# Splitting 20 weight pieces of k, r and v in the first FFN of a Griffin and RWKV-7 trunk, by way of DRAM

## The chip, the cores and the metric

The kernel runs on one core of a Trainium2 chip. The metric is the time of one execution on the device in microseconds (us); the median over runs counts. The engines are named as the profile names them: PE (TensorE, matrix products), PEld (its weight loads), DVE (VectorE), ACT (ScalarE), POOL (GpSimd) and SP (SyncE, which here only issues DMAs).

## The reference, cut to what matters

Two layers over 512 tokens of 1024 channels: a Griffin RG-LRU block, a gated conv-MLP (the first FFN, `D_FF` = 3072), an RWKV-7 time mixing, and a second FFN. The change touches the first FFN and the projections of the time mixing.

```python
def _conv_ffn(x, norm, w_up, conv_w, conv_b, w_down):
    h = _rmsnorm(x, norm)
    u = jnp.einsum('btd,df->btf', h, w_up)
    gate = _causal_dwconv(u[..., :D_FF], conv_w, conv_b)
    hid = jax.nn.gelu(gate, approximate=True) * u[..., D_FF:]
    return jnp.einsum('btf,fd->btd', hid, w_down)

def _rwkv7_block(x, norm, mix, w_rkv, ...):
    h = _rmsnorm(x, norm)
    xx = jnp.pad(h, ((0, 0), (1, 0), (0, 0)))[:, :-1] - h
    xs_rkv = jnp.stack([h + xx * mix[0], h + xx * mix[1], h + xx * mix[2]])
    rkv = jnp.einsum('sbtd,sde->sbte', xs_rkv, w_rkv)
    r, k, v = rkv[0], rkv[1], rkv[2]
...
```

## The kernel before

All products are made in float32 precision out of three products in the PE's faster float32r: every operand is split into a rounded part `hi` and a rest `lo`, and `mm3` (L54) adds `hi*hi`, `hi*lo` and `lo*hi` in PSUM. Activations are split once; the weights come from DRAM as float32 in pieces of 128 x 1024 (512 KB). `plan_weights` lists all pieces in the order of their use. `weights_load` (L161) fetches the next ones into a `raw` tile with a DMA on SP's queue (L166; for some pieces a second, summing DMA on POOL's queue, L168), `weights_split` (L172) makes `wh` on ACT (L94) and `wl` on DVE (L97), and `next_weights` hands a split piece to the product and keeps two pieces loading and one split ahead. All these tiles come from one pool `b4` of 21 buffers of 4 KB per partition, in which mixes, selections and other tiles of that size live too.

`project_gen` runs a product over four blocks of output: 8 passes of 3 matmuls for a piece in each block's turn, 24 matmuls of 512 columns a piece. After each step it calls `background`, which advances generators in the list `tasks` (three lanes) at a given rate, so that work of other stages is spread between the products.

The first FFN (`ffn(0)`, 157 to some 526 us) works on 12 pairs of 256 hidden channels. Pairs 0 to 2, 4, 6, 8 and 10 are `Whole`: four products G0, U0, G1, U1 (gate and up, halves of the 1024 inputs). Pairs 3, 5, 7, 9 and 11 are `Halves`, a form with seven products of half size (1, 5, 6, 2, 7, then 4, 3). The gate's product lands in `gpad`, of which two tiles take turns (n % 2), goes through the convolution `cv` (L688, L690) into `ge` (two buffers), and is multiplied into the hidden tile `hid`. After the products up to 7 of each divided pair a product down (`down`, L869 by way of `project`) adds four pieces of `w_down` into x, with products 4 and 3 run in between after its first piece.

The time mixing begins with the small products of `rwkv_lora` (`lwa`, `lg`), then `rwkv_lora_k` makes the first half of k (with `l2w`, `l2a` for decay and a among it) and `rwkv_krv` the second half of k, both halves of r, and part of v. Beside them `prepare` makes norms and decays in ACT and DVE (`AR`, `BK`, with small products `ssq`, `sst`, `rec`, `knb`), and `solve` inverts 32 x 32 triangles (`aab` on PE, `A`, `D`, `X` on DVE, then `XN`, `LT` and the product `m1p`). `back` is a selection matrix, transposed on PE from `sel`, which POOL fills (L1133, L1139) at the beginning of `rwkv_krv`; it is used only in `knb`. The order on each engine is set by a scheduler that places instructions by its own estimates; the order of the code gives the dependencies, and the reuse of buffers.

## Time and profile before

| what | value |
| --- | --- |
| median of 3 runs | 1293.43 us (1292.26 to 1294.64) |
| profiled execution | 1295.77 us, span 1294.1 us |
| granted PE clock, mean | 0.996 |
| stretch 157 to 526 us (first FFN): PE, DVE, ACT busy | 369.0, 256.3, 158.6 us of 369 |
| stretch 526 to 707 us (lora, k, r, first of v) | 172.6, 158.4, 113.4 us of 181 |
| stretch 707 to 870 us (chunks, product out) | 154.3, 121.4, 101.7 us of 163 |
| stretch 870 to 1294 us (second FFN) | 417.8, 271.4, 180.3 us of 424 |
| DMA: share and rate in the four stretches | 0.49, 129 GB/s; 0.27, 82; 0.21, 64; 0.44, 120 |

A stretch is read in us from the first instruction. Busy times are sums of the instructions' spans on an engine. Consecutive matmuls overlap, so that a PE that is busy all the time may still differ in how many products it makes. A wait is the idle time of an engine in front of an instruction and is put down to what ended last.

### The profile page before, as it was taken

What the parts mean: (1) busy time and instruction counts of PE and PEld (TensorE: products, weight loads), DVE (VectorE), ACT (ScalarE), POOL (GpSimd) and SP (SyncE); (2) the same over time, 40 slices, a digit from 0 to 9 for tenths busy, and PEclk for the clock granted to TensorE, in tenths of its full rate; (3) what the DMA queues carried; (4) which work ended last, traced back from release to release, by engine and by line L of the source; (5) the groups of instructions that cost most, each with busy time, mean ns of one, the idle gap of its engine ahead of it and who ended that gap; (6) DMA issues with size and microseconds to landing.
All of it is one profiled execution on the core that took longest, in us unless ns stands there. A gap on an engine that the chain in (4) does not pass through costs nothing.

```text
span 1294.1 us, 22380 instructions
## 1 busy us (share of the span) xinstructions
PE 1267.5 (98%) x9259; PEld 1069.2 (83%) x9259; DVE 931.4 (72%) x1412; ACT 664.6 (51%) x1070; POOL 104.6 (8%) x142
## 2 busy tenths in 40 slices
PE   9999999999999999999899999899999999999998
PEld 8777888989888888877678887778889898988886
DVE  5998678757666666788999867778866565666653
ACT  6797455434334343468845468655644343343432
POOL 3000001010101000010002031210010101010100
PEclk9999999999999999999999999999999999999999
DMA  7312344545454553422212122132354544545431
GB/s 222 110 58 90 98 129 100 161 100 166 95 176 85 179 99 101 157 71 76 82 38 87 51 61 83 44 99 77 107 110 148 113 162 99 171 91 178 97 133 65
DMA packets 117829, 141.37 MB, mean 109 GB/s; under 512 B 10138, under 2 KB 91748, under 8 KB 117600
## 3 DMA queue, kind: packets, MB, share of 16 engines
q1 hardware_dynamic: 100528, 122.44, 30.0%
q0 software_dynamic: 16624, 16.47, 8.4%
q8 instruction: 72, 1.18, 0.4%
q10 hardware_dynamic: 576, 1.05, 0.2%
q14 instruction: 29, 0.24, 0.1%
HBM read 135.41 MB, written 4.52 MB: 108 GB/s over the span
## 4 chain that ended last, share of the span: by engine, by line
PE 85%; DVE 8%; ACT 4%; issue 2%; POOL 0%; DMA 0%; POOLq 0%; ACTq 0%; DVEq 0%
PE acc L54 26%; PE accU L54 12%; PE accG L54 12%; PE accA L54 9%; PE accF L54 4%; PE acc L845 3%; PE acc L844 3%; PE acc L843 3%; PE accD L54 2%; DVE wl L97 1%; PE acc L1244 1%; PE s L1412 1%; DVE AR L1102 1%; DVE mt L965 1%; PE pd L1494 1%
## 5 line engine op out<-in xcount | busy, mean ns | idle before, releaser
L97 DVE TENSOR_TENSOR wl<-raw,wh 128x1024 fp32r<-128x1024 f32 (+1 forms) x161 | 195.5, 1220 | 128.1 <-ACT wh L94 107.8
L94 ACT CAST wh<-raw 128x1024 fp32r<-128x1024 f32 (+1 forms) x161 | 165.9, 1042 | 195.5 <-PE acc L54 54.5
L54 PE MATMUL accG<-xs,wh 128*128 128x512 f32 x448 | 138.8, 391 | 0.0
L54 PE MATMUL accU<-xs,wh 128*128 128x512 f32 x448 | 138.7, 391 | 0.0
L54 PE MATMUL acc<-hid,wh 128*128 128x512 f32 x384 | 119.8, 395 | 0.0
L744 DVE TENSOR_TENSOR lo<-raw,hi 128x1024 fp32r<-128x1024 f32 x70 | 85.5, 1222 | 39.4 <-PE accU L54 32.0
L743 ACT CAST hi<-raw 128x1024 fp32r<-128x1024 f32 x70 | 73.6, 1053 | 60.7 <-PE accU L54 25.3
L54 PEld LDWEIGHTS accG<-xs,wh 128*128 128x128 f32 x448 | 83.6, 188 | 17.4
L54 PEld LDWEIGHTS accU<-xs,wh 128*128 128x128 f32 x448 | 83.7, 188 | 17.1
L54 PE MATMUL accG<-xs,wl 128*128 128x512 f32 x224 | 87.3, 390 | 0.0
L54 PE MATMUL accU<-xs,wl 128*128 128x512 f32 x224 | 87.3, 390 | 0.0
L54 PEld LDWEIGHTS acc<-hid,wh 128*128 128x128 f32 x384 | 71.3, 187 | 16.7
L54 PE MATMUL accA<-xt,hi 128*128 128x256 f32 x480 | 83.4, 277 | 0.0
L54 PE MATMUL acc<-xs,wh 128*128 128x512 f32 x256 | 81.1, 399 | 0.0
L690 DVE SCALAR_TENSOR_TENSOR cv<-gpad,pv,cv 128x512 f32<-128x512 f32 x96 | 69.1, 747 | 12.3 <-ACT cv L688 11.8
L845 PE MATMUL acc<-wl,hid 128*128 128x512 f32 (+1 forms) x200 | 77.2, 386 | 0.0
L844 PE MATMUL acc<-wh,hid 128*128 128x512 f32 (+1 forms) x200 | 77.0, 385 | 0.0
L843 PE MATMUL acc<-wh,hid 128*128 128x512 f32 (+1 forms) x200 | 76.7, 383 | 0.0
L54 PE MATMUL acc<-hid,wl 128*128 128x512 f32 x192 | 75.0, 395 | 0.0
L54 PEld LDWEIGHTS accA<-xt,hi 128*128 128x128 f32 x480 | 73.2, 188 | 0.9
L54 PE MATMUL accA<-xt,lo 128*128 128x256 f32 x240 | 66.3, 276 | 0.0
L168 POOL DMA_DIRECT2D raw<-in_ffn_w_up_dram x20 | 25.7, 1287 | 478.5 <-DMA raw<-in_ffn_w_up_dram 283.6
(411 smaller groups left out, 2943.4 us busy)
## 6 DMA issues: line engine op xcount, KB each, us to landing
raw<-in_ffn_w_up_dram SPq DMA_DIRECT2D x106, 512.0 KB, 3.9
raw<-in_ffn_w_down_dram SPq DMA_DIRECT2D x48, 512.0 KB, 3.9
raw<-in_ffn_w_up_dram POOLq DMA_DIRECT2D x30, 512.0 KB, 5.9
raw<-in_rwkv_w_rkv_dram SPq DMA_DIRECT2D x24, 512.0 KB, 3.7
raw<-in_lru_w_in_dram SPq DMA_DIRECT2D x16, 512.0 KB, 4.2
raw<-in_lru_w_out_dram SPq DMA_DIRECT2D x8, 512.0 KB, 3.8
raw<-in_rwkv_w_out_dram SPq DMA_DIRECT2D x8, 512.0 KB, 3.4
xd<-x SPq DMA_DIRECT2D x8, 256.0 KB, 2.0
```

Source lines behind the costliest of these rows:

```text
L54: mm = lambda *a, **kw: self.nc.tensor.matmul(ps, *a, skip_group_check=more, **kw)
L94: put = (self.nc.vector.tensor_copy if dve else self.nc.scalar.copy)(hi, src)
L97: self.nc.vector.tensor_tensor(lo, src, hi.bitcast(F32), ALU.subtract)
L168: self.nc.gpsimd.dma_start(raw, more, accum_op=ALU.add)
L690: nc.vector.scalar_tensor_tensor(cv, pair.gp[:, e, j : j + T], cw(j), cv, ALU.mult, ALU.add)
L743: nc.scalar.copy(hi, f[p])
L744: tt(lo, f[p], hi.bitcast(F32), ALU.subtract)
L843: nc.tensor.matmul(ps, hh[:, s], wh[:, k, m], start=kk == 0, stop=False)
L844: nc.tensor.matmul(ps, hl[:, s], wh[:, k, m], start=False, stop=False)
L845: nc.tensor.matmul(ps, hh[:, s], wl[:, k, m], start=False, stop=kk == blocks - 1)
L965: nc.vector.scalar_tensor_tensor(mt[:, 1:], h[:, cb, : T - 1], self.vec("rwkv_mix", i * 8 + cb), mt[:, 1:], ALU.mult, ALU.add)
L1102: nc.vector.tensor_tensor_scan(AR[b // 4][:, b % 4, c, C : 3 * C], kp, sg[:, c * P : (c + 1) * P], 0.0, ALU.mult, ALU.add)
```

## The change

The plan marks 20 pieces as made ahead: the 8 of k, the 8 of r and the first 4 of v (`AHEAD`). A generator `split_ahead` fetches one of them per step on SP's queue into a tile `early`, splits the one fetched in the step before into `eh` (ACT) and `el` (DVE), and stores the parts split a step earlier to DRAM with two DMAs on POOL's queue. It is pushed to lane 1 in the first FFN, behind products up to 7 of pair 3, and advances by 0.19 at each of the 16 steps of a product down (3 steps in each), and by 0.25 at each of the 8 calls of a whole pair (2 in each); before the last product down the rest is done at once. Later `weights_load` takes `wh` and `wl` of such a piece from DRAM with two DMAs on POOL's queue (float32 in DRAM, float32r in the tile), and `weights_split` has nothing to do for it.

The room for `early` (2 x 4 KB) is made in the first FFN by one `gpad` and one buffer of `ge` in place of two. Around the products down, pieces are split earlier (`between`, `then`), and `back` is made in the third step of `prepare`.

```diff
--- before.py
+++ after.py
@@ -29,6 +29,8 @@
 WARM2 = 20
 WARM = 14
 
+AHEAD = 20
+
 HALVES = (3, 5, 7, 9, 11)
 
 PARAMS = [
@@ -145,6 +147,7 @@
         full(I["lru_w_in"][0], [2, 3, 0, 1])
         full(I["lru_w_out"][0], [0, 1])
         ffn(0)
+        self.ahead = range(len(plan), len(plan) + AHEAD)
         for i in (1, 0):
             full(I["rwkv_w_rkv"][0, i], [0, 1])
         for g in range(4):
@@ -155,19 +158,46 @@
                 add(I["rwkv_w_out"][0], h * 512, g * 256, 4)
         ffn(1)
         self.plan = plan
-        self.loaded, self.splitted = {}, {}
+        self.loaded, self.splitted, self.stored = {}, {}, {}
         self.n_load = self.n_split = self.n_used = 0
 
     def weights_load(self, upto):
         while self.n_load < min(upto, len(self.plan)):
             i = self.n_load
             src, k, _, more = self.plan[i]
+            if i in self.stored:
+                self.loaded[i] = tuple(self.b4(F32R, (k, D // k), f"{part}{i}") for part in ("wh", "wl"))
+                for t, d in zip(self.loaded[i], self.stored[i]):
+                    self.nc.gpsimd.dma_start(t, d)
+                self.n_load += 1
+                continue
             raw = self.b4(F32, (k, D // k), f"raw{i}")
             self.nc.sync.dma_start(raw, src)
             if more is not None:
                 self.nc.gpsimd.dma_start(raw, more, accum_op=ALU.add)
             self.loaded[i] = raw
             self.n_load += 1
+
+    def split_ahead(self, pool):
+
+        raws, parts = {}, {}
+        n = self.ahead.stop
+
+        for i in range(self.ahead.start, n + 2):
+            if i < n:
+                src, k = self.plan[i][:2]
+                raws[i] = pool.tile([P, k, D // k], F32, tag="early", name="early", bufs=2)
+                self.nc.sync.dma_start(raws[i], src)
+            if i - 2 in parts:
+                k = self.plan[i - 2][1]
+                self.stored[i - 2] = [self.dram.tile([P, k, D // k], F32, name=f"{part}d{i - 2}") for part in ("wh", "wl")]
+                for t, d in zip(parts.pop(i - 2), self.stored[i - 2]):
+                    self.nc.gpsimd.dma_start(d, t.bitcast(F32))
+            if i - 1 in raws:
+                k = self.plan[i - 1][1]
+                parts[i - 1] = [self.b4(F32R, (k, D // k), f"{part}{i - 1}") for part in ("eh", "el")]
+                self.split(raws.pop(i - 1), *parts[i - 1])
+            yield 1
 
     def weights_split(self, upto, pin=False):
         while self.n_split < min(upto, len(self.plan)):
@@ -177,6 +207,10 @@
                 continue
             self.weights_load(i + 1)
             raw = self.loaded.pop(i)
+            if i in self.stored:
+                self.splitted[i] = raw
+                self.n_split += 1
+                continue
             k = self.plan[i][1]
             hi = self.b4(F32R, (k, D // k), f"wh{i}")
             lo = self.b4(F32R, (k, D // k), f"wl{i}")
@@ -236,7 +270,7 @@
         self.const = ctx.enter_context(tc.tile_pool(name="const", bufs=1))
         self.psum = ctx.enter_context(tc.tile_pool(name="psum", bufs=1, space=PSUM))
         self.xsp = ctx.enter_context(tc.tile_pool(name="xsp", bufs=1))
-        dram = ctx.enter_context(tc.tile_pool(name="dram", bufs=1, space=DRAM))
+        dram = self.dram = ctx.enter_context(tc.tile_pool(name="dram", bufs=1, space=DRAM))
         self.xd = dram.tile([P, KB, T], F32, name="xd")
         self.tgd = dram.tile([160, T], F32, name="tgd")
         c = self.const
@@ -591,7 +625,7 @@
                 return pool.tile([P, n], dt, tag=tag, name=tag, bufs=bufs)
 
             rbs, norm = [], []
-            gpads = [pool.tile([P, 2, T + 2], F32, name=f"gpad{i}") for i in range(2)]
+            gpads = [pool.tile([P, 2, T + 2], F32, name=f"gpad{i}") for i in range(1 + l)]
             for u in gpads:
                 nc.vector.memset(u[:, :, 0:2], 0.0)
             late = []
@@ -676,12 +710,12 @@
             class Pair:
 
                 def __init__(pair, n):
-                    pair.n, pair.gp = n, gpads[n % 2]
+                    pair.n, pair.gp = n, gpads[n % len(gpads)]
                     pair.w, pair.bank, pair.s = {}, {}, {}
 
                 def gate(pair, e):
                     if not e:
-                        pair.ge = pool.tile([P, 2, T], F32, tag="ge", name="ge", bufs=2)
+                        pair.ge = pool.tile([P, 2, T], F32, tag="ge", name="ge", bufs=1 + l)
                     fb = 2 * pair.n + e
                     cv = t("cv", 2)
                     cw = lambda j: self.vec(f"ffn_conv_w{l}", j * FB + fb)
@@ -722,6 +756,7 @@
                                 tt(un, un, pair.ge[:, e], ALU.mult)
                             self.split(un, pair.hid[:, e, 0], pair.hid[:, e, 1])
                         self.background(1)
+                        self.background(0.25, 1)
 
             class Halves(Pair):
 
@@ -866,7 +901,7 @@
                             elif not g and c == pieces - 1:
                                 then()
 
-                        self.project(hids, ev, kb=blocks, join=2 if g else 1, rate=0.5 if final else 2, after=hook, x0=b0)
+                        self.project(hids, ev, kb=blocks, join=2 if g else 1, rate=0.5 if final else 2, rate1=0 if final else 0.19, after=hook, x0=b0)
 
             rooms = []
 
@@ -875,12 +910,27 @@
                     rooms.append(pool.tile([P, 2, 2, T], F32R, tag="xt", name="hx", bufs=4))
                 return rooms[-1][:, b % 2, 0], rooms[-1][:, b % 2, 1]
 
+            def between():
+                products((n, 3))
+                if n < 11:
+                    self.weights_split(self.n_used + 2)
+
+            def then():
+
+                if len(seq) > at[0]:
+                    self.weights_split(self.n_used + 2)
+                ahead(at[0] + 2)
+
             for n in range(3, 12, 2):
                 products((n, 7))
+                if n == 3 and not last:
+                    self.push(self.split_ahead(pool), 1)
                 if n == 11 and not last:
+                    while self.tasks[1]:
+                        self.background(1, 1)
                     self.norm_begin()
                     self.push(self.lora_weights())
-                down(n, 2 * n - 6, 4 if n < 11 else 8, lambda: products((n, 3)), lambda: ahead(at[0] + 2))
+                down(n, 2 * n - 6, 4 if n < 11 else 8, between, then)
             if not last:
                 after()
 
@@ -1139,11 +1189,15 @@
                     nc.gpsimd.memset(sel[hb, b, c : c + 1], 1.0)
             for b in range(KB):
                 nc.gpsimd.tensor_copy(selk[hb, b, e : e + 1], self.vec("rwkv_r_k", b)[hb])
-        psb = self.bank("back")
-        for j in range(4):
-            nc.tensor.transpose(psb[0:40, j * P : (j + 1) * P], sel[:, j, :], self.ident)
-        back = self.b4(F32R, (4 * P,), "back")[0:40]
-        nc.scalar.copy(back, psb[0:40, :])
+        backs = []
+
+        def selection():
+            psb = self.bank("back")
+            for j in range(4):
+                nc.tensor.transpose(psb[0:40, j * P : (j + 1) * P], sel[:, j, :], self.ident)
+            backs.append(self.b4(F32R, (4 * P,), "back")[0:40])
+            nc.scalar.copy(backs[0], psb[0:40, :])
+
         ppads = [pool.tile([P, NC, C + 1], F32, name=f"ppad{i}") for i in range(2)]
         for pp in ppads:
             nc.vector.memset(pp[:, :, 0:1], 1.0)
@@ -1167,6 +1221,8 @@
                 nc.scalar.activation(bytok(fac), a, AF.Identity, bias=self.oka[:, b : b + 1], scale=self.vec("rwkv_k_a", b))
                 nc.scalar.activation(pp[:, :, :, 1:], Lc, AF.Exp, scale=-DECAY_C)
                 yield 1
+                if g == 0 and j == 2:
+                    selection()
 
                 sqs.append(sq)
                 for i in (3, 0, 1, 2) if j == 3 else ():
@@ -1202,7 +1258,7 @@
                 b = g * 4 + j
                 Lc = self.inner(AR, b)
                 pb = self.bank("knb")
-                nc.tensor.matmul(pb, back[:, j * P : (j + 1) * P], rec, start=True, stop=True)
+                nc.tensor.matmul(pb, backs[0][:, j * P : (j + 1) * P], rec, start=True, stop=True)
                 nc.vector.scalar_tensor_tensor(Lc, Lc, self.nkk[:, b : b + 1], bytok(pb), ALU.mult, ALU.mult)
                 if j == 3:
                     self.done.add(("prepare", g))
```

The line numbers grow by 2 to 56 with this: L54 becomes L56, L94 and L97 become L96 and L99, L168 becomes L177, L748 becomes L783. `raw` keeps its name, and the new lines are L171 (loads of stored parts), L190 (fetch of `early`) and L195 (stores).

The first place is POOL's queue in the first FFN, from pair 3 to pair 5. Before, it holds summing transfers of divided pairs alone:

```order
L168 DMA raw_1900<-in_ffn_w_up_dram 128x4x256
L748 DMA raw_1893<-in_ffn_w_up_dram 128x4x256
L168 DMA raw_2423<-in_ffn_w_up_dram 128x4x256
L168 DMA raw_2428<-in_ffn_w_up_dram 128x4x256
L748 DMA raw_2421<-in_ffn_w_up_dram 128x4x256
```

And in the changed kernel, with the stores (`whd`, `wld` are the tiles in DRAM):

```order
L783 DMA raw_1891<-in_ffn_w_up_dram 128x4x256
L195 DMA whd_2395<-eh_2356 128x1024
L195 DMA whd_2479<-eh_2399 128x1024
L195 DMA wld_2396<-el_2357 128x1024
L195 DMA wld_2480<-el_2400 128x1024
L177 DMA raw_2439<-in_ffn_w_up_dram 128x4x256
L195 DMA whd_2573<-eh_2483 128x1024
L177 DMA raw_2444<-in_ffn_w_up_dram 128x4x256
L195 DMA wld_2574<-el_2484 128x1024
L195 DMA whd_2871<-eh_2577 128x1024
L195 DMA wld_2872<-el_2578 128x1024
L783 DMA raw_2437<-in_ffn_w_up_dram 128x4x256
```

Eight stores now stand ahead of and between the summing transfers of pair 5, where there were none.

The second place is PE at the second half of k. Before, `back` stands ahead of the first piece of that half (`acc_5265` is its first block):

```order
L54 MATMUL acc_4929<-mix,wh_5074 128x512 x2
L54 MATMUL acc_4929<-mix,wl_5075 128x512
L1144 MATMUL back<-ident,sel 40x128 x4
L54 MATMUL acc_5265<-mix,wh_5080 128x512 x2
L54 MATMUL acc_5265<-mix,wl_5081 128x512
```

In the changed kernel it stands in the second piece of that half, in front of its last block:

```order
L56 MATMUL acc_5450<-mix,wh_5270 128x512 x2
L56 MATMUL acc_5450<-mix,wl_5271 128x512
L1197 MATMUL back<-ident,sel 40x128 x4
L56 MATMUL acc_5451<-mix,wh_5270 128x512 x2
L56 MATMUL acc_5451<-mix,wl_5271 128x512
```

It has moved behind 42 products of the same half.

The third place is DVE in the same half of k, from the operand `n` of the norms to the product `knb`. Before, rows of splits (`wl`) stand between those of `prepare`:

```order
L1190 TENSOR_SCALAR n_5218<-sst 128x4x8
L1180 TENSOR_TENSOR BK_4904<-kp,fac 128x4x2x64
L97 TENSOR_TENSOR wl_5404<-raw_5395,wh_5403 128x1024
L1192 RECIPROCAL n_5218<-n_5218 128x4x8
L1174 TENSOR_TENSOR kp<-BK_4905,pinv 128x512
L1192 RECIPROCAL n_5218<-n_5218 128x4x8
L1175 SCALAR_TENSOR_TENSOR BK_4905<-BK_4905,pv,kp 128x4x128
L1177 COPY AR_4903<-ppad_5261 128x4x2x64
L1179 TENSOR_TENSOR AR_4903<-BK_4905,ppad_5261 128x4x128
L1199 TENSOR_TENSOR rec<-rec 8x512
L1177 COPY AR_4903<-ppad_5262 128x4x2x64
L97 TENSOR_TENSOR wl_5513<-raw_5401,wh_5512 128x1024
```

In the changed kernel there is none between them:

```order
L1246 TENSOR_SCALAR n_5408<-sst 128x4x8
L1231 SCALAR_TENSOR_TENSOR BK_5103<-BK_5103,pv,kp 128x4x128
L1248 RECIPROCAL n_5408<-n_5408 128x4x8
L1235 TENSOR_TENSOR AR_5101<-BK_5103,ppad_5445 128x4x128
L1248 RECIPROCAL n_5408<-n_5408 128x4x8
L1233 COPY AR_5101<-ppad_5444 128x4x2x64
L1010 TENSOR_SCALAR mt<-x,om 128x512 x2
L1015 SCALAR_TENSOR_TENSOR mt<-x,pv,mt 128x511
L1255 TENSOR_TENSOR rec<-rec 8x512
L1235 TENSOR_TENSOR AR_5101<-BK_5103,ppad_5444 128x4x128
L1262 SCALAR_TENSOR_TENSOR AR_5100<-AR_5100,nkk,knb 128x4x128 x4
```

The splits are gone from there, and more steps of the second half of `prepare` and of the next mixes stand ahead of `rec`.

## The prediction

> **What bounds the kernel now.** I read the busy times first, then the busy times by stretch, then what the PE waits for, and only then the groups of the two engines that split weights.
>
> ```profile
> PE 1267.5 (98%) x9259; PEld 1069.2 (83%) x9259; DVE 931.4 (72%) x1412; ACT 664.6 (51%) x1070; POOL 104.6 (8%) x142
> 250.00:315.00 65.00, 65.00 (x368) 56.54 (x366) 42.91 (x54) 25.84 (x32) 3.79 (x3) 1.00 0.50 133
> 550.00:707.00 157.00, 148.59 (x943) 115.62 (x943) 142.48 (x270) 104.01 (x187) 14.42 (x51) 0.99 0.24 73
> 630.00:640.00 10.00, 8.39 (x62) 4.91 (x64) 9.74 (x14) 5.68 (x10) 2.29 (x2) 0.88 0.34 105
> 640.00:650.00 10.00, 10.00 (x136) 7.84 (x130) 8.18 (x15) 7.57 (x19) 0.00 (x0) 0.95 0.17 54
> ```
>
> The first line is that of the profile's page; the others give, for a stretch, its length and then PE, PEld, DVE, ACT and POOL busy, the granted clock, the DMA share and GB/s. The PE sets the time nearly everywhere. In the first FFN (250 to 315 us) it is busy for 65.00 of 65.00 us, while DVE has 22 us and ACT 39 us to spare. From 550 to 707 us (products of k, r and the first of v) the PE lacks 8.4 of 157 us and DVE is the fullest engine beside it, 142.5 of 157. So the splits stand in the one stretch where DVE is scarce, and the change carries them to one where it is not. What that is worth is not DVE's time but the PE's waits:
>
> ```profile
> PE acc L54 <- ACT wh L94: 2.5, 2, 2.0
> PE back L1144 <- POOL sel L1139: 2.1, 1, 2.1
> PE aab L1275 <- DVE AR L1206: 1.4, 1, 1.4
> PE rbc L338 <- POOL rs L334: 0.9, 1, 0.9
> PE acc L54 <- DVE wl L97: 0.5, 1, 0.5
> PE knb L1205 <- DVE rec L1199: 0.2, 1, 0.2
> PE l2a L1097 <- DVE l2l L97: 0.2, 1, 0.2
> PE m1p L1322 <- DVE XN L1303: 1.1, 1, 1.1
> L97 DVE TENSOR_TENSOR wl<-raw,wh 128x1024 fp32r<-128x1024 f32 x18 | 23.0, 1277 | 3.0 <-ACT wh L94 3.0
> L94 ACT CAST wh<-raw 128x1024 fp32r<-128x1024 f32 x19 | 19.6, 1047 | 3.1 <-PE acc L54 3.0
> ```
>
> The first eight rows are all the waits of the PE between 524 and 716 us (us in total, times, longest); the last two are the groups of the splits between 550 and 707 us. Waits of 8.9 us are all that this stretch holds.
>
> **The change, part by part.** *Splits taken out.* Of the 20 pieces two are split before 550 us and 18 after it, those 18 by 23.0 us of DVE and 18 x 1.047 = 18.8 us of ACT. The waits on `wh` and `wl` (2.5 + 0.5 = 3.0 us) go with them, for PE then waits for a load instead. The four waits on other work of DVE (`aab` 1.4, `m1p` 1.1, `knb` 0.2, `l2a` 0.2, together 2.9 us) shrink: DVE is relieved of 23.0 us, the PE comes at most some 7 us earlier. Nothing shows that all of them vanish, since each hangs on a chain over ACT and PE too; between 0 and 2.9 us I take 2.0. The wait for `rs` (0.9 us) stays, and is late next.
>
> *Selection moved.*
>
> ```profile
> 603.91 0.23 POOL L1133 MEMSET sel<- 128x160 f32 x1 [26.11 <-DMA tgd<-lf]
> 604.25 0.69 POOL L1139 MEMSET sel<- 64x1 f32 x16
> 654.88 14.51 PE acc L54 x62
> ```
>
> The two POOL rows (start, length) make `sel`, late because its room is free only when `tgd` is stored; the PE waits 2.1 us for it. The last row, of the chain that ended last, prices a 512-column product at 14.51 / 62 = 0.234 us. In the new order 42 more of these stand ahead of `back`, 9.8 us, so the 2.1 us go and 7.7 us are left in hand. The cover is less than that by what the POOL queue adds ahead of `sel`, the loads of the first seven pieces.
>
> *Loads in place of raw pieces.* Each of the 20 pieces costs two 512 KB loads on POOL's queue instead of one on SP's.
>
> ```profile
> L1716 POOL DMA_DIRECT2D fg<-in_final_norm_dram x1: 578/578/578, 1229.9 to 1229.9; - x1
> L168 POOL DMA_DIRECT2D raw<-in_ffn_w_up_dram x20: 1261/1277/1384, 196.4 to 1206.4; - x20
> raw<-in_rwkv_w_rkv_dram SPq DMA_DIRECT2D x24, 512.0 KB, 3.7
> fg<-in_final_norm_dram POOLq DMA_DIRECT2D x1, 512.0 KB, 6.1
> ```
>
> The first two rows give POOL's time for an issue (ns, least, median, most); the others the time from issue to landing (us). The one transfer of this shape on POOL, 128 rows of 4 KB, cost POOL 0.578 us and landed after 6.1. A pair lands after about 6.1 + 0.6 = 6.7 us, against 3.7 + 1.05 + 1.28 = 6.0 us for fetch and split before: no dearer, with pieces asked for two pieces ahead, 2 x 24 x 0.234 = 11.2 us of PE work. POOL gains 80 x 0.578 = 46 us of issues in some 400 us: it is idle for most of that time, and nothing on the path waits for it but `rs`, `sel`, the identity `X` and `LT`, each of which now has loads in front. Bounds for this part: 0, and 2 us (the waits for `rs` and `sel` once more, 0.9 + 2.1, less what the move hides); I take 0.
>
> The Trainium skill, "GPSIMD Engine Reference", section "Key points", speaks against this part: POOL shares its SBUF interfaces with DVE, with contention when DVE reads two operands from SBUF, which is what most of DVE's work is here. By that rule an issue would stretch where DVE is dense; the trace disagrees so far, for the 20 issues of L168 lie between 1261 and 1384 ns. I keep it as a rival below.
>
> *What the first FFN gets.* Per pair of pairs (about 63 us) five steps: on ACT 5 x 1.05 and on DVE 5 x 1.28 = 6.4 us, into 22 us that are free; SP gets five fetches, POOL ten stores. One buffer each of `gpad` and `ge` goes: they are rewritten only after the next pair's G products, 2 x 24 x 0.234 = 11 us of PE work behind the last U product of the pair before, whose readers are done by then, so I count nothing. The DMA engines are the narrow place:
>
> ```profile
> 315.00:378.00 63.00, 63.00 (x359) 54.95 (x357) 40.91 (x51) 24.29 (x30) 3.81 (x3) 1.00 0.51 131
> 325.70:329.86 4.16, 4.16 (x19) 3.34 (x18) 0.83 (x2) 1.05 (x1) 0.00 (x0) 1.00 1.00 156
> 365.57:371.17 5.60, 5.60 (x27) 4.52 (x26) 2.98 (x4) 1.84 (x3) 0.00 (x0) 1.00 0.81 277
> ```
>
> They are busy for 0.51 x 63 = 32 us of a period now. Plain traffic ran at 277 / 0.81 = 342 GB/s of full use; the stretch with a summing transfer at 156 GB/s with the engines full. Five steps move 7.86 MB: at 342 GB/s 23 us, so 55 of 63 us. That still fits, but what it delays matters in one spot, the first piece of a product down:
>
> ```profile
> 357.17 6.94 SPq L166 DMA_DIRECT2D raw<-in_ffn_w_down_dram  x4
> 360.89 1.05 ACT L94 CAST wh<-raw 128x1024 fp32r<-128x1024 f32 x1 [0.30 <-DMA raw<-in_ffn_w_down_dram]
> 361.98 1.23 DVE L97 TENSOR_TENSOR wl<-raw,wh 128x1024 fp32r<-128x1024 f32 x1 [3.61 <-ACT wh L94]
> 365.41 0.62 PE L54 MATMUL acc<-hid,wh 128*128 128x512 f32 x2
> raw<-in_ffn_w_down_dram SPq DMA_DIRECT2D x48, 512.0 KB, 3.9
> xd<-x SPq DMA_DIRECT2D x8, 256.0 KB, 2.0
> ```
>
> It is fetched at 357.17, split by 363.21 and used at 365.41: 2.2 us in hand, four times (pairs 5, 7, 9, 11). No step is made during the five products of a divided pair before it, so most stores are over by then. A transfer in front of it at 342 GB/s costs 1.5 us, less than the 2.2. Bounds: 0, and the overload of the second rival; I take 0.5 us, near the 0 that these rows give.
>
> The Trainium skill, "DMA: Bandwidth & Descriptors", section "Queues, rings and completion order", says that each DMA engine takes turns between the queues that have work. By this SP's fetch keeps half of each engine beside POOL's stores and loses at most its own 1.5 us; the term would be 0 instead of 0.5. No row here shows the two queues full at once.
>
> *Sum.* -3.0 - 2.0 - 2.1 + 0.5 = **-6.6 us**. The profiled execution took 1295.77 us (span 1294.1), which gives 1289.2; it lies 2.3 us above the median of the runs, 1293.43, and against that median it is **1286.8 us**.
>
> **The rivals.** *The splits were hidden anyway.* The PE is busy for 98%; behind each wait on `wh` stands the next link, a mix or an `AR`, and the wait comes back under another name. Only `sel` goes: 1293.4 - 2.1 = 1291.3. For it: ACT's chain of `prepare` is as long as before. Against it: both engines that make these links lose a sixth of their work there.
>
> *Stores crowd the DMA engines in the first FFN (slower).* Place: the first piece of each product down, and from there all the weights. It decides at one number: over 2.2 us of delay the PE stands, four times; at (7.1 / 4) + 2.2 = 4.0 us the gain is spent, at 4.6 us (landing after 8.5 us instead of 3.9) the kernel is slower by 0.2%. If stores ran like the summing transfer, 156 GB/s, a period would need 32 + 5.24 / 0.156 = 34, + 8 for fetches, 74 us in 63: 4 x 11 us more, 1330 us. A delay of 6 us gives 1293.4 - 7.1 + 4 x 3.8 = 1301.5. For it: the stretch at share 1.00 exists already, just where the steps are put. Against it: `xd`, the store that the trace has, lands 256 KB in 2.0 us.
>
> *More falls than the waits.* All 8.9 us go but `rs`, and with them the lower clock from 630 to 650 us (0.12 x 10 + 0.05 x 10 = 1.7 us) and about 1 us of restarts: 1293.4 - 8.0 - 2.7 = 1282.7.
>
> *POOL's issues stretch under DVE.* If an issue took twice 0.578 us, the seven pairs ahead of `sel` would cost 8 us more and eat the 7.7 in hand; the 2.1 us come back: 1288.9.
>
> **How the numbers follow.** Forecast 0.51, hidden 0.18, crowded 0.13, more 0.14, stretched 0.04. The range from 1281.5 to 1294.5 takes in the forecast, the hidden, the stretched and nearly all of the third case, and of the crowded one only its mildest part; some 0.15 are left out. A measurement tells 0.2% (2.6 us) from nothing: faster means under 1290.8, slower over 1296.0. Faster: 0.51 + 0.14 + 0.04 and a little of the hidden, 0.70; within 0.2% 0.17; slower 0.13.
>
> **What would show it.** Right: from 524 to 716 us no PE wait on `wh`, `wl` or `sel`, DVE some 23 us less busy, and the first FFN still 65 of 65 us. Wrong: PE waits in the first FFN, behind a landing of `in_ffn_w_down` over 6 us or a split that stands behind a late `early`; in the second stretch PE waits on `DMA wh` or `DMA wl`, or on POOL; a DMA share near 1.00 over a whole period.

## The result, and the profile after

The changed kernel takes **1327.74 us** (median of 4 runs, 1326.99 to 1329.81), the kernel before 1293.11 us (4 runs, 1292.26 to 1294.64) beside it: a ratio of 1.0261, 95% interval [1.0249, 1.0274], or 34.6 us slower. The forecast was 1286.8 us. Two of the runs below had one slow execution each (e10_own_pinned 4391.73 us, e12_act_queue 1418.00 us), and their medians are of the other executions. The first fence has the busy times of the page of after, then its busy times by stretch (length; PE, PEld, DVE, ACT, POOL; granted clock, DMA share, GB/s): two stretches that the prediction showed of before, and three beside them.

```profile
PE 1278.2 (96%) x9259; PEld 1077.4 (81%) x9259; DVE 932.2 (70%) x1411; ACT 663.4 (50%) x1070; POOL 145.0 (11%) x222
250.00:315.00 65.00, 57.92 (x299) 49.75 (x298) 41.72 (x51) 25.95 (x32) 8.32 (x11) 0.95 0.70 206
315.00:378.00 63.00, 54.57 (x282) 45.94 (x281) 40.07 (x48) 24.61 (x31) 9.30 (x13) 0.98 0.77 238
378.00:442.00 64.00, 60.92 (x306) 51.90 (x306) 38.06 (x46) 22.99 (x27) 8.00 (x12) 0.94 0.69 214
442.00:526.00 84.00, 74.83 (x415) 64.91 (x413) 55.06 (x67) 33.80 (x41) 10.64 (x14) 0.96 0.71 211
600.00:707.00 107.00, 107.00 (x585) 82.84 (x588) 91.45 (x183) 72.13 (x130) 21.75 (x64) 1.00 0.46 141
```

The first FFN had the PE busy all the time before. Now it is idle for 3 to 9 us in every period, and the granted clock is 0.94 to 0.98 of full: it falls after each standstill. The time mixing is the reverse, full at a clock of 1.00. Two rows of the groups that read `mix` fix how much each gives; the first is before, the second after (first and last start of k's, r's and the first of v's products):

```profile
L54 PE MATMUL acc<-mix,wh x192: 387/389/504, 572.3 to 688.7; 128*128 128x512 f32 x192
```

```profile
L56 PE MATMUL acc<-mix,wh x192: 387/389/499, 619.4 to 726.4; 128*128 128x512 f32 x192
```

k begins 47.1 us later. From there to the first gate product of the second FFN it took 325.9 us (898.2 - 572.3) and takes 312.9 (932.3 - 619.4), 13.0 less; the second FFN is the same. A part of both has nothing to do with the steps: without them (e0_bystanders, below) k begins at 575.0 us and the time from there is 321.3, so 44.4 us of the loss and 8.4 us of the gain are theirs. The loss is in the first FFN. The gain in the time mixing is real, and larger than forecast. The waits of the PE between 250 and 620 us in after (us in total, times, longest):

```profile
PE accA L56 <- ACT s L800: 22.2, 4, 6.6
PE accU L56 <- ACT wh L96: 6.5, 3, 2.6
PE accU L56 <- DVE wl L99: 2.0, 4, 0.5
PE rbc L372 <- POOL rs L368: 0.9, 1, 0.9
PE acc L56 <- DVE wl L99: 0.3, 1, 0.3
```

30.7 us in front of `accA` and `accU`, one long wait in each period; with the clock (3.3 + 1.3 + 3.8 + 3.4 = 11.7 us, each stretch times what it lacks to 1.00) that is 42.4 of the 47.1 us. `s L800` is ACT's copy of `accA`, and it is late because ACT does its work in order. What stands in front of it is told by the chain of waits of one such standstill (start, us, what):

```profile
418.98 8.62 DMA raw<-in_ffn_w_up_dram
...
428.20 0.50 POOL raw L177
...
428.98 1.07 POOL wld L195
430.05 9.27 issue
...
439.32 3.23 DMA whd<-eh
...
442.62 0.07 ACT hi L778
...
446.55 1.24 DVE lo L779
...
447.80 4.29 DMA raw<-in_ffn_w_up_dram
...
452.17 1.04 ACT hi L778
453.22 0.49 ACT s L800
...
453.76 2.29 PE accA L56 x9
```

Two things are to be seen. A weight piece took 8.62 us to land, where 3.8 to 3.9 was usual. And ACT's `hi`, main work, begins when the **store** `whd<-eh` has landed: it writes into the room that `eh` had. The same is to be seen from ACT's and POOL's timeline (start, length, in brackets the idle time before and what ended it), just ahead of that, and from the groups of ACT's casts between 250 and 530 us:

```profile
434.14 1.04 ACT L96 CAST wh<-raw 128x1024 fp32r<-128x1024 f32 x1 [9.92 <-DMA whd<-eh]
437.99 1.04 ACT L96 CAST eh<-early 128x1024 fp32r<-128x1024 f32 x1 [1.85 <-DMA wld<-el]
```

```profile
425.20 1.31 POOL L177 DMA_DIRECT2D raw<-in_ffn_w_up_dram  x1 [11.71 <-DMA raw<-in_ffn_w_up_dram]
425.97 1.10 POOL L195 DMA_DIRECT2D whd<-eh  x1
```

```profile
L96 ACT CAST wh<-raw 128x1024 fp32r<-128x1024 f32 x28 | 29.4, 1051 | 88.6 <-PE acc L56 30.8 <-DVE raw L772 21.2 <-DMA whd<-eh 18.4
L96 ACT CAST eh<-early 128x1024 fp32r<-128x1024 f32 x19 | 19.5, 1046 | 14.2 <-DMA wld<-el 14.2
```

The store asked for at 425.97 stood in POOL's queue behind a summing transfer that had waited 11.71 us for its own piece, landed at 434.1, and ACT stood 9.92 us for it. `b4` is one pool of 21 rooms for raw pieces, `wh`, `wl`, `hi`, `lo` and now `eh` and `el` (my expectations call it a ring). Which tile gets which room is fixed in the compiled program, and there 29 of the 40 rooms of `eh` and `el` go next to a tile of the main work, 4 to 11 tiles later; the other 11 go to the `eh` of the next step, and for those ACT, which works in order, stands 14.2 us more. The chain that ended last goes through the landing of a store in every period (from 276.05, 335.89, 411.82, 439.32 and 516.49 us).

DMAs between 250 and 530 us, first before, then after (KB each, median us from issue to landing):

```profile
raw<-in_ffn_w_up_dram SPq DMA_DIRECT2D x32, 512.0 KB, 3.8
raw<-in_ffn_w_down_dram SPq DMA_DIRECT2D x20, 512.0 KB, 3.8
raw<-in_ffn_w_up_dram POOLq DMA_DIRECT2D x12, 512.0 KB, 5.9
```

```profile
raw<-in_ffn_w_up_dram SPq DMA_DIRECT2D x34, 512.0 KB, 6.4
whd<-eh POOLq DMA_DIRECT2D x19, 512.0 KB, 3.4
wld<-el POOLq DMA_DIRECT2D x19, 512.0 KB, 6.3
raw<-in_ffn_w_down_dram SPq DMA_DIRECT2D x14, 512.0 KB, 3.7
raw<-in_ffn_w_up_dram POOLq DMA_DIRECT2D x12, 512.0 KB, 8.0
```

Pieces of `w_up` and summing transfers land 2 to 3 us later, pieces of `w_down` do not. Rooms that stores hold, or bytes that crowd the engines: the experiments had to part these.

### The profile page after: what moved, and what is told of

Its sections match the earlier page's. It is cut to its first block, busy times and chain, and to the rows that moved or that the text cites. A ratio compares the mean times of both kernels' runs of the same rounds, so it can differ in the third digit from the quotient of the medians.

```text
span 1328.1 us, 22593 instructions
## 1 busy us (share of the span) xinstructions
PE 1278.2 (96%) x9259; PEld 1077.4 (81%) x9259; DVE 932.2 (70%) x1411; ACT 663.4 (50%) x1070; POOL 145.0 (11%) x222
## 4 chain that ended last, share of the span: by engine, by line
PE 73%; issue 12%; DMA 6%; DVE 5%; ACT 3%; POOL 1%; SPq 0%; POOLq 0%; ACTq 0%; DVEq 0%
PE acc L56 24%; PE accU L56 8%; PE accG L56 8%; PE accA L56 7%; DMA raw<-in_ffn_w_up_dram 3%; PE acc L880 3%; PE acc L879 3%; PE acc L878 3%; PE accF L56 3%; DMA wld<-el 2%; PE accD L56 2%; PE lg L56 1%; PE s L1468 1%; PE acc L1300 1%; DVE X L1354 1%
## 5 line engine op out<-in xcount | busy, mean ns | idle before, releaser
L96 ACT CAST wh<-raw 128x1024 fp32r<-128x1024 f32 (+1 forms) x141 | 145.6, 1042 | 185.9 <-DMA raw<-in_ffn_w_down_dram 38.4
L99 DVE TENSOR_TENSOR wl<-raw,wh 128x1024 fp32r<-128x1024 f32 (+1 forms) x141 | 170.3, 1213 | 79.5 <-ACT wh L96 76.0
L56 PE MATMUL accU<-xs,wh 128*128 128x512 f32 x448 | 141.0, 396 | 6.5 <-ACT wh L96 6.5
L56 PE MATMUL accG<-xs,wh 128*128 128x512 f32 x448 | 138.7, 391 | 0.0
L56 PE MATMUL acc<-hid,wh 128*128 128x512 f32 x384 | 120.2, 397 | 0.0
L56 PE MATMUL accA<-xt,hi 128*128 128x256 f32 x480 | 92.2, 294 | 22.2 <-ACT s L800 22.2
L56 PEld LDWEIGHTS accU<-xs,wh 128*128 128x128 f32 x448 | 84.8, 191 | 25.1 <-ACT wh L96 7.9
L56 PEld LDWEIGHTS accA<-xt,hi 128*128 128x128 f32 x480 | 79.7, 203 | 23.9 <-ACT s L800 23.0
L56 PEld LDWEIGHTS accG<-xs,wh 128*128 128x128 f32 x448 | 83.7, 188 | 17.3
L56 PE MATMUL accU<-xs,wl 128*128 128x512 f32 x224 | 89.0, 397 | 2.0 <-DVE wl L99 2.0
L56 PE MATMUL accG<-xs,wl 128*128 128x512 f32 x224 | 87.3, 390 | 0.0
L56 PEld LDWEIGHTS acc<-hid,wh 128*128 128x128 f32 x384 | 71.6, 188 | 16.8 <-ACT wh L96 0.3
L56 PE MATMUL acc<-xs,wh 128*128 128x512 f32 x256 | 81.1, 399 | 0.0
L56 PE MATMUL acc<-hid,wl 128*128 128x512 f32 x192 | 75.2, 397 | 0.3 <-DVE wl L99 0.3
L56 PE MATMUL accA<-xt,lo 128*128 128x256 f32 x240 | 69.9, 291 | 0.0
L722 ACT ACTIVATE cv<-gpad,pv 128x512 f32<-128x512 f32 x48 | 38.0, 811 | 56.5 <-DVE gpad L809 37.5
```

What stands on the lines that cost most here:

```text
L56: mm = lambda *a, **kw: self.nc.tensor.matmul(ps, *a, skip_group_check=more, **kw)
L96: put = (self.nc.vector.tensor_copy if dve else self.nc.scalar.copy)(hi, src)
L99: self.nc.vector.tensor_tensor(lo, src, hi.bitcast(F32), ALU.subtract)
L722: nc.scalar.activation(cv, pair.gp[:, e, 0:T], AF.Identity, bias=self.vec(f"ffn_conv_b{l}", fb), scale=cw(0))
```

## The experiments

All results first. "k" is the start of k's first product in the profiled execution, "mixing" from there to the second FFN. Without steps k begins at 575.0 us with 21 rooms and at 576.7 with 20; what a run lies above that is its loss in the first FFN.

| run | median us | ratio to before [95%] | k | mixing |
| --- | --- | --- | --- | --- |
| after | 1327.74 | 1.0261 [1.0249, 1.0274] | 619.4 | 312.9 |
| e0_bystanders | 1295.20 | 1.0004 [0.9993, 1.0015] | 575.0 | 321.3 |
| e1_stored_unused | 1338.83 | 1.0337 [1.0320, 1.0354] | 616.0 | 322.1 |
| e2_no_store | 1294.47 | 0.9999 [0.9990, 1.0009] | 574.1 | 322.0 |
| e3_traffic | 1318.66 | 1.0180 [1.0161, 1.0199] | 594.5 | 327.4 |
| e5_ring20 | 1299.29 | 1.0041 [1.0027, 1.0056] | 576.7 | 327.8 |
| e8_own_rooms | 1329.47 | 1.0276 [1.0254, 1.0298] | 609.5 | 321.7 |
| e6_at_once | 1329.08 | 1.0267 [1.0252, 1.0283] | 616.9 | 312.7 |
| e7_spread | 1323.43 | 1.0226 [1.0209, 1.0243] | 612.6 | 313.4 |
| e9_thin_stores | 1322.18 | 1.0212 [1.0193, 1.0232] | 600.9 | 321.0 |
| e10_own_pinned | 1304.58 | 1.0078 [1.0061, 1.0095] | 586.0 | 320.2 |
| e11_half | 1303.05 | 1.0064 [1.0047, 1.0081] | 587.8 | 316.3 |
| e12_act_queue | 1340.36 | 1.0348 [1.0328, 1.0368] | 630.0 | 314.7 |
| e13_pinned | 1336.28 | 1.0320 [1.0305, 1.0334] | 623.9 | 313.7 |
| e14_own_thin | 1306.34 | 1.0084 [1.0068, 1.0099] | 580.0 | 327.6 |
| e15_in_place | 1323.16 | 1.0217 [1.0203, 1.0231] | 611.2 | 312.8 |
| e16_in_place_half | 1293.65 | 0.9990 [0.9981, 0.9998] | 578.3 | 317.1 |
| e17_own_10 | 1290.63 | 0.9969 [0.9956, 0.9981] | 574.8 | 317.9 |
| e17_own_14 | 1288.50 | 0.9955 [0.9942, 0.9969] | 575.6 | 314.6 |

### Which part of the change costs

**e0_bystanders.** The line `self.push(self.split_ahead(pool), 1)` is taken out.

> The changed kernel without its 20 steps: nothing is fetched, split or stored ahead, and all pieces of k, r and v are split in time mixing as before. Left of the change are one buffer each of gpad and ge in the first FFN, the splits that stand around the products down, and the selection further back. Theory rooms (what costs 47 us in the first FFN is that rooms of the b4 ring wait for stores to land) and theory crowding (the DMA engines are full): no cost here, 1291 us (before 1293.1 less the 2.1 us of the selection). Theory bystanders (the lost buffers cost it): a part of the 47 us shows here, 1300 us or more.

No difference: the lost buffers of `gpad` and `ge` cost nothing. The 2.1 us of the selection did not come either: the wait on `sel` is gone, but the PE's wait on `wh` in time mixing is 3.5 us in place of 2.5, and those on DVE for `bon` and `knb` are 1.6 and 1.2 us in place of 0.5 and 0.2. All the PE's waits between 524 and 760 us are 9.7 us, 9.8 before.

**e1_stored_unused.** `self.stored[i - 2] = [...]` becomes `self.unused[i - 2] = [...]`.

> The first FFN as in the changed kernel, with fetches, splits and stores, but time mixing takes the raw pieces and splits them itself as before: the stored parts are not used. All theories: the first FFN loses its 47 us again and time mixing gains only the selection's 2.1 us, 1338 us (1293.1 + 47.4 - 2.1). If the halves depend on each other, it is another figure: under 1333 would say that the loads of the stored parts have a share in the 47 us or that the gain in time mixing was the first FFN's lateness made good.

1338.8, as expected: the halves are independent. Using the stored parts is worth 1338.8 - 1327.7 = 11.1 us by the medians and 322.1 - 312.9 = 9.2 us by the time mixing of the profiled executions; making them costs 41 us (616.0 - 575.0).

**e2_no_store.** The two stores of a step are taken out, with the use of their parts.

> Fetches and splits of the 20 steps stay in the first FFN, their rooms in the b4 ring too, but nothing is stored, and time mixing splits the raw pieces again. A room is free as soon as its split is done. Theory rooms: 1291 to 1295 us. Theory crowding: two thirds of the added bytes are gone (the stores), 1291 to 1305 us. Theory bystanders, or the work of ACT and DVE on the splits: 1325 us or more.

Nothing is lost. Fetches, splits and even the rooms of `eh` and `el` are free as long as nothing is stored from them; whether it is the hold or the bytes of the stores that costs, this run does not tell. One stretch of it:

```profile
315.00:378.00 63.00, 63.00 (x357) 55.08 (x356) 46.08 (x55) 29.47 (x34) 3.81 (x3) 1.00 0.62 171
```

DVE and ACT have 5.2 us more to do each than before, and the PE stays at 63 of 63. Between 250 and 530 us the pieces of `w_up` landed after 6.2 us here, almost as late as in after (6.4), and the PE lost nothing by it.

**e3_traffic.**

```
-                for t, d in zip(parts.pop(i - 2), self.stored[i - 2]):
+                for t, d in zip(full, self.unused[i - 2]):
...
-                self.split(raws.pop(i - 1), *parts[i - 1])
+                parts[i - 1] = raws.pop(i - 1)
```

Here `full` is two parts of `sums[0]`, a tile that stands unchanged; nothing is split, and the stored parts are not used.

> The traffic of the 20 steps alone: the same fetches into their own two buffers and 40 stores of 512 KB on POOL's queue at the same places, from a tile that stands unchanged through the first FFN. No split, no room of the b4 ring, no wait for a store; time mixing splits the raw pieces again. Theory rooms: 1291 to 1296 us. Theory crowding: the whole loss without the gain, 1330 to 1338 us.

Neither: k begins 19.5 us late (594.5 - 575.0), and the run wasn't what I meant it to be. With nothing to wait for, the fetches and stores ran ahead and came in one burst:

```profile
170.00:250.00 80.00, 61.75 (x296) 52.25 (x295) 52.95 (x84) 34.22 (x54) 18.85 (x31) 0.90 1.03 346
```

It shows what 80 us of full DMA engines cost (18 us of PE time), and nothing on five steps in a period.

### Bytes or rooms: first try

**e5_ring20.** `N4 = 20`, no steps.

> No steps, as in the first run (e0_bystanders), and the b4 ring has 20 rooms instead of 21. It prices the room that the next run takes from the ring. Theory rooms: a missing room costs where the ring is short, 0 to 8 us, 1295 to 1303 us. Theory crowding: nothing, 1295 us.

4.4 us more than the kernel before (1299.29 against 1294.86 beside it), in time mixing (327.8 against 321.3); in the first FFN a missing room costs 1.7.

**e8_own_rooms.** Stores right behind the split, `N4 = 20`, and

```
-  parts[i - 1] = [self.b4(F32R, (k, D // k), f"{part}{i - 1}") for part in ("eh", "el")]
+  parts[i - 1] = [pool.tile([P, k, D // k], F32R, tag="eh", name="eh", bufs=1), raws[i - 1].bitcast(F32R)]
```

> All 20 steps with fetch, split, store and the loads in time mixing, the same bytes on the same queues at the same products, but out of the b4 ring: eh has a room of its own, el is written over the fetched piece, the ring gives up one room (20) for it, and the stores are asked for right behind the split. No split or load of the main work can wait for a store any more. Theory rooms: the loss in the first FFN goes and the gain in time mixing stays, 1280 to 1288 us, plus what the run with 20 rooms costs. Theory crowding: the loss stays, 1320 us or more.

By the figure, crowding. But again the steps had run ahead, all of them between 155 and 330 us: from 157 to 250 us the DMA share is 0.91, and from 378 us on the PE is full again. The rooms of `b4` had also been what paced the steps.

**e6_at_once.** The stores move up behind `self.split(...)`.

> The changed kernel with one thing moved: the stores are asked for right behind their split instead of a step later; eh and el are in the b4 ring (21 rooms) as before. Rooms come free a step earlier (7 us at a product down, some 30 us across the products of a divided pair), the bytes are the same. Theory rooms: at least half of the loss goes, 1285 to 1305 us. Theory crowding: 1320 us or more.

Nothing changed, because on the chip nothing had moved. In after POOL asks for a store 0.3 us after its cast wherever nothing stands ahead (cast from 361.25 to 362.30, store at 362.60), and here too (359.95 to 361.00, 361.29): the scheduler had put the stores right behind their splits already. So this run says nothing on how long a room may be held.

**e7_spread.** Both rates 0.131, and `self.background(0.131, 1)` in the products of divided pairs too.

> The changed kernel with its five steps of a period spread evenly over it, the products of the divided pairs included (0.131 of a step at each of 38 places in place of three in a product down and two in a whole pair). Fetch, split and store stay a step apart, so a pair of rooms is held for 12 us and a store's landing at each step. Theory rooms: the waits for rooms stay, 1315 us or more. Theory crowding: the engines are full nowhere (51 of 63 us at the rates seen), 1281 to 1300 us.

4 us better than after, no more. That speaks against crowding by the mean load. But the waits for stores are nearly gone as well: between 250 and 530 us ACT waits 0.3 us for one (34.8 in after), and 67.6 us for weight pieces that come late (21.5 in after). Neither theory was whole by now.

### The two apart

**e9_thin_stores.** As e1_stored_unused, with `t[0:16]` stored in place of `t`.

> The run e1_stored_unused with one difference: a store moves only 16 of its 128 rows, 64 KB instead of 512, so the 40 stores carry an eighth of their bytes. As there, time mixing does not use the stored parts. Number, place and queue of the stores, the rooms of eh and el and the step for which they are held are as before. Theory crowding (the bytes of the stores fill the DMA engines, and the weights of the first FFN land late): the loss goes, 1291 to 1298 us. Theory rooms and order (what waits is the room held for a step, or POOL's queue with the summing transfers behind the stores): most of e1_stored_unused's loss stays, 1318 us or more.

26 us of the 41 are left with an eighth of the bytes. Its DMAs between 250 and 530 us, and ACT's waits there:

```profile
whd<-eh POOLq DMA_DIRECT2D x20, 64.0 KB, 2.5
raw<-in_ffn_w_up_dram POOLq DMA_DIRECT2D x12, 512.0 KB, 7.7
```

```profile
ACT wh L96 <- DMA whd<-eh: 28.3, 4, 8.0
```

A thin store lands in 2.5 us, and ACT's `wh` still waits four times up to 8.0 us for one, since it stands in POOL's queue behind the summing transfer, which waits for its piece. So 26 us are not the bytes of the stores but the hold of their rooms, with what stands ahead of them in the queue; the bytes make it 41.

**e10_own_pinned.** e8_own_rooms with `keep_in_program_order` around fetch, cast and store, so that five steps stand in each period.

> The run e8_own_rooms, where the steps had run ahead to 160 to 340 us, with each fetch, split and store kept in program order on its engine, so that five steps stand in each period as in the changed kernel. No load or split of the main work needs a room that a store holds. Theory crowding: the loss stays, 1318 us or more. Theory rooms: 1283 to 1295 us, the gain in time mixing less the 4.4 us that 20 rooms cost and a little.

The loss is 9.3 us (586.0 - 576.7): all bytes of the change, no shared room. Now the prediction's place shows, PE `acc` behind a late `wh` of a piece of `w_down`, and its size:

```profile
PE acc L56 <- ACT wh L96: 4.8, 4, 1.8
PE acc L56 <- DVE wl L99: 1.6, 3, 0.5
PE accA L56 <- ACT s L798: 1.6, 2, 1.1
```

**e11_half.** `AHEAD = 10`, all rates 0.0655, in the products of divided pairs too, rooms in `b4`.

> Ten pieces (the eight of k, the first two of r) instead of 20, at half the rate, spread evenly over the period (0.0655 of a step at each place): some 2.5 steps in a period, rooms in the b4 ring as in the changed kernel. Half the gain in time mixing, 5.5 us. Theory crowding: 42 of 63 us of the DMA engines are used instead of 51, and the loss is less than half of the loss with 20, 1288 to 1302 us. Theory rooms: each step costs what it did, 2.3 us, half of the 47 us stays: 1310 us.

12.8 us lost, 1303: at the border of both, and it parts nothing.

**e12_act_queue.** `self.nc.scalar.dma_start` in place of `self.nc.gpsimd.dma_start` for the stores.

> The changed kernel with its 40 stores asked for by ACT on its own queue instead of by POOL; everything else is the same, the loads in time mixing are POOL's as before. The summing transfers are then alone on POOL's queue in the first FFN. Theory crowding: the same bytes, 1318 us or more. Theory order (the summing transfers wait behind stores in POOL's queue): 1283 to 1300 us.

Worse, 1340.4. ACT's waits for stores are gone (0.3 us between 250 and 530), and the loss is greater all the same: it waits 84.4 us for weight pieces. Of the DMAs between 250 and 560 us:

```profile
raw<-in_ffn_w_up_dram SPq DMA_DIRECT2D x34, 512.0 KB, 9.0
```

### Rooms or order

e10_own_pinned had changed the rooms and the order. The next four part these.

**e13_pinned.** The changed kernel with `keep_in_program_order` alone.

> The changed kernel with each fetch (SP), cast (ACT) and store (POOL) of the 20 steps kept in program order on its engine, and nothing else: eh and el in the b4 ring with 21 rooms, stores a step after their split. Theory order (the scheduler's order, three fetches in a row behind five weight pieces, is what costs): the loss ahead of time mixing falls to the 9 us of e10_own_pinned, k's first product at 584 us, 1292 to 1300 us in all. Theory rooms (weights wait for rooms that stores hold): it stays near 40 us, k at 612 us or later, 1318 us or more.

The order alone isn't it: 49 us are lost, where own rooms lose 9 in nearly the same order (there the stores stand right behind the split). The wait has another place here, and is as long, and ACT waits only 6.8 us for a store:

```profile
PE accU L56 <- ACT wh L96: 24.0, 4, 7.5
```

**e14_own_thin.** e10_own_pinned with thin stores, not used.

> The run e10_own_pinned with thin stores of 64 KB instead of 512; time mixing splits the raw pieces again and does not use the stored parts. Theory that the remaining 9 us of e10_own_pinned are bytes: k's first product at 577 to 579 us as with 20 rooms and no steps, 1299 to 1302 us. Theory that they are the splits, the waits of SP and POOL or the order: k at 583 us or later, 1306 us or more.

Between the two: 3.3 us are left, so 6 of the 9.3 were bytes.

**e15_in_place.** It differs from e10_own_pinned in two lines:

```
-  N4 = 20
+  N4 = 21
-  parts[i - 1] = [pool.tile([P, k, D // k], F32R, tag="eh", name="eh", bufs=1), raws[i - 1].bitcast(F32R)]
+  parts[i - 1] = [self.b4(F32R, (k, D // k), f"eh{i - 1}"), raws[i - 1].bitcast(F32R)]
```

> Program order kept as in e13_pinned, stores right behind their split, el written over the fetched piece and only eh in the b4 ring of 21 rooms: one room of the ring in a step instead of two, and for a shorter time. All 20 pieces. Theory order: as e10_own_pinned without its 20 rooms, 1292 to 1300 us. Theory rooms: half of the rooms, about half of the 41 us: k at 592 to 600 us, 1303 to 1312 us.

The cleanest pair: the same order, the same bytes, one room more, and 36 us lost (611.2) in place of 9.3, by `eh` alone in the pool. It is more than the half that I expected: the loss doesn't go by the count of rooms. And no wait of ACT for a `whd` or `wld` store is left. What the chain shows in place of it (near 490 us, then two groups of waits between 250 and 530 us):

```profile
483.98 4.90 DMA wld<-early
...
488.93 0.37 SPq L190
...
489.40 0.58 SPq L175
...
490.62 7.96 DMA raw<-in_ffn_w_up_dram
```

```profile
SPq L190 <- DMA wld<-early: 125.4, 14, 17.5
ACT eh L96 <- DMA early<-in_rwkv_w_rkv_dram: 41.8, 5, 9.2
```

SP's fetch of the next `early` (L190) waits until the store from that tile has landed, the fetches of `w_up` (L175) come behind it in SP's order, and ACT's pinned cast of `eh` waits for such late fetches. e10_own_pinned has both waits too, 99.5 and 21.1 us.

**e16_in_place_half.** The same with `AHEAD = 10` and rates of 0.0655, in the products of divided pairs too.

> As e15_in_place with ten pieces at half the rate, spread evenly (0.0655 of a step at each place). Gain in time mixing about 5 us. Theory order: a loss of at most 3 us ahead of time mixing, 1289 to 1294 us, level with before or a little faster. Theory rooms: 10 us lost, 1299 to 1303 us.

The number is the one that the other theory gave: 3.3 us lost. So the price is not per room: with half the steps, twice as far apart and spread evenly, it is nearly gone.

### All rooms left to the main work

**e17_own_10, e17_own_14.** All 21 rooms for the main work; one room for the fetched piece (`el` over it), one for `eh`; a step in two halves, spread evenly (0.131 and 0.184 of a half step at each place).

```
+  raw = pool.tile([P, k, D // k], F32, tag="early", name="early", bufs=1)
+  pin(self.nc.sync.dma_start(raw, src))
+  yield 1
+  parts = [pool.tile([P, k, D // k], F32R, tag="eh", name="eh", bufs=1), raw.bitcast(F32R)]
+  self.split(raw, *parts, pin=True)
...
+      pin(self.nc.gpsimd.dma_start(d, t.bitcast(F32)))
+  yield 1
```

> Ten pieces, all 21 rooms of b4 left to the main work: the fetched piece has one room of its own, eh another, el is written over the fetched piece, and the next fetch is asked for half a step after the stores. Program order kept, steps spread evenly. Theory rooms: nothing is lost ahead of time mixing, k's first product at 575 to 577 us, time mixing 317 us as in e16_in_place_half, 1290 to 1292 us. Theory that bytes and steps cost by themselves: as e16_in_place_half, k at 578 us or later, 1293.5 us.

> The same with 14 pieces at 1.4 times the rate; 1.4 times the gain of stored pieces in time mixing, 315.5 us. Theory rooms: k at 575 to 578 us, 1288.5 to 1291.5 us. Theory that bytes and steps cost by themselves: more than 1.4 times the loss of the run with ten, k at 580 us or later, 1294 us or more.

Nothing is lost any more (574.8 and 575.6 us), and both beat the kernel before: 1290.63 us, 0.9969 [0.9956, 0.9981], and 1288.50 us, 0.9955 [0.9942, 0.9969]. The first FFN of the run with 14 pieces:

```profile
250.00:315.00 65.00, 65.00 (x366) 56.66 (x365) 45.52 (x56) 28.07 (x34) 7.16 (x9) 1.00 0.70 201
315.00:378.00 63.00, 63.00 (x357) 55.07 (x356) 43.99 (x54) 27.96 (x34) 8.22 (x11) 1.00 0.76 224
378.00:442.00 64.00, 64.00 (x361) 55.86 (x360) 45.14 (x56) 27.68 (x33) 7.15 (x9) 1.00 0.74 211
442.00:526.00 84.00, 83.01 (x441) 70.72 (x440) 61.98 (x79) 36.44 (x46) 7.68 (x10) 1.00 0.64 180
```

The DMA share, 0.64 to 0.76, is about that of after (0.69 to 0.77), and the PE stands for 1.0 us instead of 30.7. A share of 0.7 does not cost by itself. Against e16_in_place_half the run with 10 pieces differs in the room of `eh` and in the half step, and 3.3 us of loss become none. With 20 pieces and all 21 rooms no run was made.

## Why the prediction was wrong

**The step that failed** is "What the first FFN gets", taken as +0.5 us; it measured +44 (619.4 - 575.0). The step counted the work of the engines and the bytes, and both fit, as it said: the splits cost nothing (e2_no_store), and the mean DMA share stayed at 0.77 or under, below the forecast 55 of 63 us (0.87). It didn't count rooms, nor what stands in order behind the added transfers. `eh` and `el` are of the pool that the weights of the first FFN live in, and a room of theirs comes free not with the split but when POOL has reached the store and the store has landed. "Most stores are over by then" held well enough for the one place that I had priced, the first piece of a product down: pieces of `w_down` landed after 3.7 us in the median, and the PE waits 0.3 us for them in all. The PE waited in the products of whole and divided pairs, where main work had been planned into the room just stored.

The traces show this way of the loss in the changed kernel, in e1_stored_unused, e6_at_once and e9_thin_stores: 33 to 42 us of ACT's waits between 250 and 530 us end with the landing of a store. They do not show it for e7_spread, e12_act_queue, e13_pinned and e15_in_place, which lose 36 to 55 us with 0 to 7 us of such waits; there weight pieces or fetches of `early` come late. That the shared pool is at fault rests on the pair e10_own_pinned and e15_in_place. How a room of the pool turns into a late weight is shown for the first group of runs only.

**The rival of crowding** had the sign and, with 1330 us, the time, but the time by luck, for its price is wrong: stores don't run at the 156 GB/s of a summing transfer (415 GB/s together with fetches in e3_traffic). Crowding is there, and smaller: some 6 of 9.3 us with own rooms (e10_own_pinned less e14_own_thin), and some 15 of 41 in the shared pool, where a longer landing holds a room longer (e1_stored_unused less e9_thin_stores). Its place, `acc` behind a late piece of `w_down`, shows only with rooms of their own (e10_own_pinned).

**Splits taken out and the waits on DVE**, -3.0 and -2.0: right in kind, too small. Between 570 and 760 us the waits on `wh`, `wl`, `aab`, `m1p`, `knb` and `l2a` are gone but for 0.3 us on `wl`, in the last product down; the one for `rs`, 0.9 us, stayed, as forecast. With the granted clock at 1.00 the use of stored parts gives 9.2 to 11.1 us. My third rival had 8.0 + 2.7 = 10.7, from the same rows; but 2.1 of that were for `sel`, which is not in what was measured, and about 1 us was for restarts, which no run shows by themselves. **Selection moved**, -2.1: nothing by itself (e0_bystanders); for that edit the rival "hidden anyway" held, the wait came back as longer waits on `wh`, `bon` and `knb`. **Loads in place of raw pieces**, 0: right; the pairs landed in 4.4 and 5.0 us, and the PE waits for none. **One buffer each of `gpad` and `ge`**, nothing: right.

**POOL's issues and SP's fetches.** POOL's issues did not stretch: between 250 and 530 us a summing issue took 1297 ns in the median, 1268 before, and the loads of stored parts took 532 and 533 ns each, where I had counted 578. The contention that the Trainium skill names ("GPSIMD Engine Reference", "Key points") is no more than 2% in these issues. SP's pieces of `w_up` landed after 3.8 us before, after 6.2 in e2_no_store, after 6.4 in after, and after 9.0 with the stores on ACT's queue. So it is not the stores on POOL's queue that delay them from 3.8 to 6.4, for without any store they are as late; the fetches of `early` are in SP's own queue. From the turns between queues (the Trainium skill, "DMA: Bandwidth & Descriptors", "Queues, rings and completion order") I had drawn that SP's fetch loses at most 1.5 us to the stores. The 0.2 us between e2_no_store and after do not speak against that rule, and the 9.0 us of e12_act_queue, where the fetches of `early` also waited longer for the split before them (161.7 us in all, 86.0 in after), can't settle it.

**What stays open**: why half the rooms cost 36 us at five steps a period and 3 at half that (e15_in_place, e16_in_place_half). The planned order of the rooms does not tell these two apart: in the compiled programs the room of `eh` goes next to a tile of the main work for 19 of 20 and for 9 of 10 pieces, 6 to 14 and 6 to 11 tiles later. SP does: its fetches of `early` wait 125.4 us for a store in the one and 0.4 us in the other. That points to a rival that no run tested, the place of these fetches ahead of the fetches of `w_up` in SP's queue; a version with the fetches of `early` on another queue was not made. Nor was one that keeps rooms and order and only moves the summing transfers, which would say how much of the 26 us of thin stores is POOL's queue.

## What to carry to other kernels

A tile that is stored holds its room until the store has landed, and what its queue has in front of it counts too; in a pool that the main work shares, that wait can land on the main work, and neither engine time nor DMA share shows it beforehand. Before adding such a tile, ask who is planned into its room next, and what stands behind its fetch in the same queue; if it is the bound engine's supply, give the tile rooms of its own, and keep what the shared pool had paced at its pace. And price a change of this kind by its stores: here fetch and split of 20 pieces were free.

## What the runs showed of the hardware

- Stores and fetches together ran at 415 GB/s in the burst of e3_traffic (250 to 270 us, share 1.03), 2.7 times the 156 GB/s of the stretch with a summing transfer at share 1.00.
- A standstill of the PE costs more than itself: in after the granted clock was 0.66 from 300 to 310 us and 0.76 from 370 to 380, where long waits ended, and 1.00 in stretches of 10 us without a wait near them. By the clock of each stretch that is 11.7 us in all, beside 30.7 us of waits.
